# Ten projection steps beside the scan, window attention and latent keys beside latent attention, and low parts of weights by an adding DMA

## The chip, the cores and the metric

One core of a Trainium2 chip runs the whole kernel as one program. The metric is device time in microseconds, the median of three runs. The engines are named as the profile names them: PE (TensorE, matrix products), DVE (VectorE), ACT (ScalarE), POOL (GpSimd), and SP, whose queue issues most DMAs. POOL issues DMAs too.

## What is computed

A two-layer encoder over 1024 tokens of 1024 features, all in float32. Cut to what matters here:

```python
for i in range(DEPTH):
    u = h @ w_in[i]
    (cq, ckv, kr, hy_u, sq, sk, sv, ssd_z, ssd_xbc, ssd_dt) = jnp.split(u, IN_OFFSETS, axis=-1)
    y_a = mla_mixer(cq, ckv, kr, ...)          # latent attention
    y_b = hyena_mixer(hy_u, ...)               # short convolution, two long convolutions with gates
    y_c = swa_mixer(sq, sk, sv, swa_sink[i])   # window attention
    y_d = ssd_mixer(ssd_xbc, ssd_dt, ...) * jax.nn.silu(ssd_z)   # state-space scan with its gate
    y = group_rms_norm(jnp.concatenate([y_a, y_b, y_c, y_d], -1), mix_norm_g[i], 4)
    h = layer_norm(ALPHA * h + y @ w_out[i], ...)
    # then the MLP and a per-layer embedding, each with its norm
```

## The kernel before

Products are made in float32 of reduced width, three for one: an operand is split into a high part (ACT copies it with rounding) and a low part (the operand less its high part, on DVE or POOL), and a product is high x high, high x low, low x high. `split` at line 92 does that, `load_w` (line 112) loads a weight on SP into the tile `wraw` (two buffers) and splits it into `wh` and `wl` (tag `whl`, four buffers, so two pairs).

The input projection is done in tiles of 128 features (`in_proj`, line 564): 48 products of 128x128 by 128x512 each, into a PSUM tile of two banks (`pp`, two buffers). The tiles are cut into two steps each. `proj` in `mixers` runs through 20 of them: six for Hyena, five for the scan's inputs (the sixth was made at the head), SV, SK, two SQ for window attention, two CQ and one CKV for latent attention (`latent`, line 615, with a gain and sums of squares), and two gates Z. Each result goes to DRAM and is read again by its mixer.

A mixer is a Python generator, and `interleave` (line 43) emits several of them in step with one another, by the number of steps that is given beside each. The scheduler of the language then orders each engine's instructions, with that emission as its priority. Three stages follow one another in each layer, in `mixers` (line 579):

- Hyena (54 steps) beside the projection (42 steps); the projection's low parts are made by POOL.
- The scan `ssd` (44), window attention `swa` (32) and the keys and values of latent attention `mla_keys` (50, of which the first 34 do nothing).
- Latent attention `mla` (40) beside the first loads of the output projection (`out_ahead`, 36).

Memory between the stages is shared: pools are opened and closed as a stack, from the left and from the right, and a tile waits for the tiles that had its place. The eight tiles of 8 KB with the tag `X` hold the layer's input, as high and low parts, until the last projection tile is done. After that the scan's inputs and states (lines 824 to 832) and the latent keys `kT` take their place. Window attention scores, its transposed probabilities and latent attention's scores all use the PSUM tile of two banks.

Of the kernel before, what the change touches and what calls it, by code (L numbers as in the profile page):

```python
# [28 lines left out]
# columns of the packed per-layer parameters  # L29
# [4 lines left out]
# feature tiles of the input projection  # L34
# [8 lines left out]
def interleave(*flows):  # L43
    """Emits flows, each (generator, number of its steps), in step with one another."""
    live = [[g, 0, n] for g, n in flows]
    while live:
        f = min(live, key=lambda f: f[1] / f[2])
        try:
            next(f[0])
            f[1] += 1  # L50
        except StopIteration:
            live.remove(f)


def stagger(items):
    """Emits the stages of items so that each item is one stage behind the one before it."""
# [18 lines left out]
class Trunk:  # L75
# [16 lines left out]
    def split(self, hi, lo, src, eng=None):  # L92
        self.act(hi, src)
        self.tt(lo, src, r(hi), ALU.subtract, eng)

# [16 lines left out]
    def load_w(self, src, shape, pool=None, tag="whl", eng=None, bufs=None):  # L112
# [7 lines left out]
        self.split(hi, lo, raw, eng or nc.gpsimd)  # L120
        return hi, lo

# [23 lines left out]
    def to_x_after(self, x, H, t0, t1, ins, pair=False):  # L146
        """Transposes token tiles t0 to t1, once the products up to ins have freed the tiles that the
        result goes to."""
# [11 lines left out]
    def layer_norm(self, h, gb, eps=None, first=None):  # L160
        """The statistics; returns two functions that normalise h in place, one after the other."""
# [16 lines left out]
        def affine(c=512):  # L178
            """The first c columns, scaled already, on GpSimd, the others on VectorE."""
# [74 lines left out]
    def embed(self):  # L254
        """Normalises the input; the second half of the tokens only when the function that is returned runs."""
# [43 lines left out]
    def sin_of(self, fp, out, pre):  # L299
        """out = sin(pre) with the argument brought to [-pi, pi]."""  # L300
# [99 lines left out]
    def bruun(self, pool, zm, zp, C):  # L400
        """Residues of a polynomial of 1024 coefficients (8 blocks of 128 rows, C columns each)
        modulo the eight factors of x^2048 - 1 of degree 256; zm and zp are its residues modulo
        x^1024 - 1 and x^1024 + 1."""
# [36 lines left out]
    def conv_fft(self, l, n, pool, z, feature_major, out):  # L440
        """Circular convolution of z (token-major, 8 x 256) with filter n, and the skip term that the
        filter holds; the result is token-major [128, 8 * 256] or feature-major [128, 2, 8 * 128]."""
# [102 lines left out]
    def in_start(self, l, tile_i, eng=None):  # L545
# [5 lines left out]
        else:  # L551
            w = self.load_w(self.t["w_in"][l, tile_i], [128, 8, 128], eng=eng)
        return w, self.two()

    def in_half(self, x, w, ps, hf):
        c0 = hf * 512
        if not isinstance(w, tuple):
            # the products of the high and the low parts of the weights, in separate rows
# [5 lines left out]
    def in_proj(self, l, x, tile_i):  # L564
        """One tile of 128 features, [128, 1024] in PSUM, in two steps."""
        w, ps = self.in_start(l, tile_i)
# [6 lines left out]
    def conv3(self, out, ps, cw):  # L573
        """Centred 3-tap convolution along the free dim with bias: cw columns w0, w1, w2, b."""
# [4 lines left out]
    def mixers(self, l, x, mu, late, st0):  # L579
# [6 lines left out]
        res, sw = {}, ExitStack()  # L586
        ss = self.sm.tile([128, 4, 8], F32, name="ss")

        def scalars(su, ps):
            """Rotary key and dt, token-major."""  # L590
# [24 lines left out]
        def latent(pr, ti, k, rs, last, n):  # L615
            """A latent of attention with its gain, to DRAM; the sums of its squares go to rs."""
# [16 lines left out]
        def proj(pr, su, head, v, x1):  # L633
# [42 lines left out]
            for i in range(2):  # L676
                yield from plain(pr, T_SQ + i, qd[:, i])
                yield
            for i in range(2):
# [4 lines left out]
            yield from latent(pr, T_CKV, 2, res["rk"], True, 128)  # L684
            yield
            for i in range(2):
                yield from plain(pr, T_Z + i, zd[:, i], AF.Silu)
                yield
# [23 lines left out]
        with ExitStack() as ssu:  # L712
            with ExitStack() as st:
# [14 lines left out]
                interleave((hyena(st, v, x1), 54), (proj(pr, su, head, v, x1), 42))  # L728
            m1 = self.pool(st0, f"m1_{l}")
            w2 = self.pool(sw, f"w2_{l}", 2, side=RIGHT)  # L730
            att = {}
            with ExitStack() as st:
                mc = self.pool(st, f"mc{l}", 2)
                interleave((self.ssd(l, st, res["scal"], xbc, zd, yd[3]), 44), (self.swa(l, w2, yd[2], qd, kd, vd), 32),
                           (self.mla_keys(l, mc, m1, att, cd, res), 50))
            sw.close()
        rows, ahead = {}, {}
# [14 lines left out]
        with ExitStack() as sa:  # L752
            m2 = self.pool(sa, f"m2_{l}", 2)
            interleave((self.mla(l, m2, att, yd[0]), 40), (out_ahead(), 36))
        return yd, ss, rows, ahead

    def token_sums(self, sq):
        """Sums over features of the tiles sq [128 features, 512 tokens], as [128, 4] with tokens on partitions."""
# [5 lines left out]
    def squares(self, ss, g, hf, y, sq):  # L764
        """For the sums of squares of group g for 512 tokens, whose features are y, tokens on partitions:
        returns the function that finishes them on the tensor engine."""
# [6 lines left out]
    def ssd_scalars(self, l, mu, dtr):  # L773
# [5 lines left out]
        # softplus(x) = max(x, 0) + log1p(exp(-|x|)), the log by its series in e / (2 + e)  # L779
# [32 lines left out]
        # log(dt) - acs  # L812
# [6 lines left out]
    def ssd(self, l, ss, scal, xbc, zd, yd):  # L819
        nc = self.nc  # L820
        Ah, Al, lg, w, dec, dsum, eacs = scal
        res = {}
# [981 lines left out]
```

## Time and profile before

| | us |
|---|---|
| median of 3 runs | 3237.84 |
| lowest and highest run | 3234.51, 3241.9 |
| span of the profiled execution | 3236.6 |
| stage of Hyena and projection, first layer | 341 |
| stage of scan, window attention and keys | 137 |
| stage of latent attention | 135 |

An engine's busy time in a stretch is the time in which at least one of its instructions ran. The granted clock is a share of TensorE's full 2.4 GHz: 1.0 is full speed, 0.5 is its lower level, and a figure in between is a mean over the stretch.

### The profile page before, as it was taken

How to read it: one execution, taken by the hardware profiler on the slowest of the kernel's cores; microseconds unless marked ns; L12 is line 12 of the kernel's file. 1: busy time of each engine (PE TensorE's matmuls, PEld its weight loads, DVE VectorE, ACT ScalarE, POOL GpSimd, SP SyncE). 2: the span in 40 equal slices, each digit the busy share in tenths (PEclk: the TensorE clock that was granted, in tenths of full speed). 3: DMA queues.
4: the chain of work that ended last, by engine and by line, in shares of the span. 5: the costliest groups of instructions: out<-in, count | busy, mean ns of one | idle time of the engine just before them, and what ended most of it. 6: DMA issues, size and time to landing. Idle time of an engine off the chain costs nothing.

```text
span 3236.6 us, 40462 instructions
## 1 busy us (share of the span) xinstructions
PE 2976.9 (92%) x14316; PEld 2429.1 (75%) x14316; DVE 2451.0 (76%) x3711; ACT 1292.0 (40%) x2278; POOL 1821.3 (56%) x1371
## 2 busy tenths in 40 slices
PE   6999989998999999999989998899989999989996
PEld 4887866877777777777868877778777777767685
DVE  7678776878765557999777786778786555689986
ACT  4332365743333334333343323667333333343341
POOL 5455533527656556886435454345177555578855
PEclk9999998999999999999999998999999999999998
DMA  5566523022222225313335755130222222343232
GB/s 178 156 200 204 192 75 130 16 83 85 85 79 78 78 79 198 123 47 115 126 100 172 225 192 165 53 121 25 97 85 79 79 78 78 114 163 107 74 135 92
DMA packets 140468, 368.98 MB, mean 114 GB/s; under 512 B 15139, under 2 KB 42023, under 8 KB 140009
## 3 DMA queue, kind: packets, MB, share of 16 engines
q1 hardware_dynamic: 126008, 315.72, 28.8%
q0 software_dynamic: 14256, 50.67, 5.2%
q8 instruction: 114, 1.87, 0.2%
q14 instruction: 90, 0.73, 0.1%
HBM read 278.77 MB, written 87.56 MB: 113 GB/s over the span
## 4 chain that ended last, share of the span: by engine, by line
PE 39%; DVE 21%; POOL 16%; issue 10%; DMA 10%; ACT 4%; SPq 0%; POOLq 0%; DVEq 0%; ACTq 0%
PE ps L99 18%; PE pp L99 13%; POOL w L87 5%; DMA wraw<-in_ffn_w_gate_dram 4%; POOL wraw L87 4%; DVE part L87 3%; POOL u L87 2%; DVE fr L87 2%; POOL H L87 2%; PE ps L942 2%; DVE H L90 2%; DVE s L87 1%; POOL part L87 1%; DVE H L87 1%; DMA wraw<-in_ffn_w_up_dram 1%
## 5 line engine op out<-in xcount | busy, mean ns | idle before, releaser
L99 PE MATMUL ps<-x,w 128*128 128x512 f32 x2112 | 508.2, 394 | 11.3 <-ACT v L84 6.1
L99 PEld LDWEIGHTS ps<-x,w 128*128 128x128 f32 x2112 | 400.1, 190 | 99.1 <-ACT v L84 7.0
L99 PE MATMUL pp<-x,wh 128*128 128x512 f32 x1344 | 427.9, 397 | 1.8 <-ACT wh L84 1.8
L99 PE MATMUL ps<-xq,w 128*128 128x512 f32 x1584 | 391.1, 397 | 29.7 <-DVE u L87 24.3
L1582 PE MATMUL ps<-part 128*128 128x512 f32 x1440 | 351.2, 399 | 33.8 <-DVE H L87 10.8
L99 PEld LDWEIGHTS ps<-xq,w 128*128 128x128 f32 x1584 | 292.9, 188 | 117.2 <-DVE u L87 50.7
L1582 PEld LDWEIGHTS ps<-part 128*128 128x128 f32 x1440 | 270.9, 191 | 110.5 <-DVE H L87 20.3
L99 PEld LDWEIGHTS pp<-x,wh 128*128 128x128 f32 x1344 | 254.9, 192 | 54.3 <-ACT wh L84 2.0
L87 POOL TENSOR_TENSOR w<-wraw,w 128x512 fp32r<-128x512 f32 x164 | 217.5, 1345 | 116.0 <-ACT w L84 116.0
L99 PE MATMUL pp<-x,wl 128*128 128x512 f32 x672 | 266.5, 397 | 3.8 <-POOL wl L87 3.8
L84 ACT ACTIVATE w<-wraw 128x512 fp32r<-128x512 f32 x264 | 151.8, 622 | 268.0 <-DMA wraw<-in_ffn_w_up_dram 218.6
L87 POOL TENSOR_TENSOR wl<-wraw,wh 128x1024 fp32r<-128x1024 f32 (+2 forms) x61 | 152.8, 2507 | 182.7 <-ACT wh L84 124.2
L87 POOL TENSOR_TENSOR part<-fr,part 128x512 fp32r<-128x512 f32 x120 | 192.4, 1628 | 47.2 <-ACT part L84 42.2
L87 DVE TENSOR_TENSOR s<-wraw 128x512 f32<-128x512 f32 x44 | 55.4, 1259 | 202.2 <-DMA wraw<-in_ffn_w_gate_dram 199.8
L99 PE MATMUL ps<-wo,yn 128*128 128x512 f32 x768 | 189.7, 405 | 5.4 <-DVE H L90 3.0
L1039 POOL TENSOR_TENSOR P<-P,smr 128x1024 f32<-128x1024 f32 x64 | 121.1, 1893 | 112.2 <-DVE smr L1038 103.3
L99 PEld LDWEIGHTS ps<-wo,yn 128*128 128x128 f32 x768 | 147.1, 195 | 39.4 <-DVE H L90 4.8
L90 DVE SCALAR_TENSOR_TENSOR g<-g,pp 128x1023 f32<-128x1023 f32 x88 | 126.6, 1439 | 57.7 <-ACT g L84 57.7
L87 POOL TENSOR_TENSOR u<-u,g 128x512 f32<-128x512 f32 x44 | 78.7, 1788 | 152.5 <-ACT g L84 152.3
L87 DVE TENSOR_TENSOR part<-wr,part 128x512 fp32r<-128x512 f32 x124 | 158.2, 1299 | 4.8 <-ACT part L84 4.8
L99 PE MATMUL ps<-wh,x 128*128 128x512 f32 x512 | 158.8, 391 | 0.0
L99 PEld LDWEIGHTS pp<-x,wl 128*128 128x128 f32 x672 | 128.5, 191 | 30.5 <-POOL wl L87 4.7
(381 smaller groups left out, 7038.7 us busy)
## 6 DMA issues: line engine op xcount, KB each, us to landing
c_fwd<-in_c_fwd_dram POOLq DMA_DIRECT2D x64, 512.0 KB, 5.1
wraw<-in_ffn_w_up_dram SPq DMA_DIRECT2D x50, 512.0 KB, 3.5
wraw<-in_ffn_w_gate_dram SPq DMA_DIRECT2D x44, 512.0 KB, 4.5
f<-u SPq DMA_DIRECT2D x88, 256.0 KB, 2.0
wraw<-in_w_in_dram SPq DMA_DIRECT2D x42, 512.0 KB, 4.1
fr<-f SPq DMA_DIRECT2D x40, 512.0 KB, 4.5
wr<-in_ffn_w_down_dram SPq DMA_DIRECT2D x36, 512.0 KB, 6.4
c_inv<-in_c_inv_dram POOLq DMA_DIRECT2D x32, 512.0 KB, 5.0
```

The lines of the kernel that those rows point to most:

```text
L84: self.nc.scalar.activation(out, in_, func, **kw)
L87: (eng or self.nc.vector).tensor_tensor(out, a, b, op=op)
L90: return self.nc.vector.scalar_tensor_tensor(out, a, s, b, op0=op0, op1=op1)
L99: ins = self.nc.tensor.matmul(out, a, b, start=i == 0, stop=i == n - 1)
L942: ins = self.nc.tensor.matmul(out[0:64] if j else out, v[:, 0, :] if j else v.rearrange("p i d -> p (i d)"), terms[i][1 + j], start=k == 0 ...
L1039: nc.gpsimd.tensor_tensor(P, P, sm.to_broadcast([128, T]), op=ALU.mult)
L1582: nc.tensor.matmul(ps, u, v, start=k == 0 and (p != 1 or ch == 0), stop=k == 5 and (p != 1 or ch == last))
```

## The change

Three things are done.

- The five tiles Z, CKV and CQ (ten steps) leave `proj`, and a new flow `proj_late` (10) makes them beside the scan (44), the gates first. The scan's inputs and states get a pool of their own, since the tag `X` still holds the projection's operands.
- Window attention (now 44) and the latent keys, which are now the first part of a flow `attention` (48) with latent attention behind them, stand beside `out_ahead` (36). The 34 empty steps of `mla_keys` are gone.
- In all projection tiles but the first two of Hyena's, the low part is made without POOL's arithmetic: ACT writes the high part, then its negative into the low part's tile, and a DMA that POOL issues adds the weight to that from DRAM.

```diff
+    def split_added(self, hi, lo, src, far):
+        self.act(hi, src)
+        self.act(lo, src, scale=-1.0)
+        self.nc.gpsimd.dma_start(lo, far, accum_op=ALU.add)
@@ load_w(..., far=False)
-        self.split(hi, lo, raw, eng or nc.gpsimd)
+        if far:
+            self.split_added(hi, lo, raw, src)
+        else:
+            self.split(hi, lo, raw, eng or nc.gpsimd)
@@ in_proj
-        w, ps = self.in_start(l, tile_i)
+        w, ps = self.in_start(l, tile_i, far=tile_i not in (T_HY, T_HY + 1))
@@ mixers, end of proj
+        def proj_late(pr):
+            for i in range(2):
+                yield from plain(pr, T_Z + i, zd[:, i], AF.Silu)
+                yield
+            yield from latent(pr, T_CKV, 2, res["rk"], True, 128)
+            yield
             for i in range(2):
                 yield from latent(pr, T_CQ + i, i, res["rq"], i, 256)
                 yield
             rq = res["rq"]
             nc.vector.tensor_scalar(rq, rq, 96.0 ** -0.5, None, op0=ALU.mult)
-            yield from latent(pr, T_CKV, 2, res["rk"], True, 128)
-            yield
-            for i in range(2):
-                yield from plain(pr, T_Z + i, zd[:, i], AF.Silu)
-                yield
@@ mixers, the three stages
-                interleave((hyena(st, v, x1), 54), (proj(pr, su, head, v, x1), 42))
-            m1 = self.pool(st0, f"m1_{l}")
-            w2 = self.pool(sw, f"w2_{l}", 2, side=RIGHT)
-            att = {}
-            with ExitStack() as st:
-                mc = self.pool(st, f"mc{l}", 2)
-                interleave((self.ssd(l, st, res["scal"], xbc, zd, yd[3]), 44), (self.swa(l, w2, yd[2], qd, kd, vd), 32),
-                           (self.mla_keys(l, mc, m1, att, cd, res), 50))
-            sw.close()
+                interleave((hyena(st, v, x1), 54), (proj(pr, su, head, v, x1), 32))
+            with ExitStack() as st:
+                interleave((self.ssd(l, st, res["scal"], xbc, zd, yd[3]), 44), (proj_late(self.pool(st, f"pl{l}", 2)), 10))
         rows, ahead = {}, {}
+        def attention(mc, m1, m2):
+            att = {}
+            yield from self.mla_keys(l, mc, m1, att, cd, res)
+            yield from self.mla(l, m2, att, yd[0])
...
         with ExitStack() as sa:
+            w2 = self.pool(sa, f"w2_{l}", 2, side=RIGHT)
+            m1 = self.pool(sa, f"m1_{l}")
+            mc = self.pool(sa, f"mc{l}", 2)
             m2 = self.pool(sa, f"m2_{l}", 2)
-            interleave((self.mla(l, m2, att, yd[0]), 40), (out_ahead(), 36))
+            interleave((attention(mc, m1, m2), 48), (self.swa(l, w2, yd[2], qd, kd, vd), 44), (out_ahead(), 36))
@@ ssd
+        sb = self.pool(ss, f"sb{l}")
         for j in range(3):
-            pair = self.xp.tile([128, 2, T], F32, name="xbc", tag="X")
+            pair = sb.tile([128, 2, T], F32, name=f"xbc{j}")
...
-            prev.append(self.xp.tile([128, 8, 2, 128], F32, name="prev", tag="X"))
-            xt.append(self.xp.tile([128, 8, 2, 128], F32, name="xt", tag="X"))
+            prev.append(sb.tile([128, 8, 2, 128], F32, name=f"prev{g}"))
+            xt.append(sb.tile([128, 8, 2, 128], F32, name=f"xt{g}"))
@@ mla_keys
-        for _ in range(34):
-            yield
```

## Rows read from the trace of the kernel before

**Rows 1.** The page's part 1: busy time of each engine, share of the span.

```profile
PE 2976.9 (92%) x14316; PEld 2429.1 (75%) x14316; DVE 2451.0 (76%) x3711; ACT 1292.0 (40%) x2278; POOL 1821.3 (56%) x1371
```

**Rows 2.** Windows, by stage: stretch, length, busy us, clock, DMA share, GB/s.

```profile
core 0: us, PE busy (x) PEld busy (x) DVE busy (x) ACT busy (x) POOL busy (x), PEclk, DMA share, GB/s
62.00:403.00 341.00, 320.37 (x1694) 275.51 (x1694) 257.94 (x361) 115.08 (x164) 171.22 (x130) 0.96 0.57 183
403.00:540.00 137.00, 117.64 (x647) 90.19 (x645) 99.49 (x332) 84.94 (x255) 48.53 (x48) 0.93 0.25 79
540.00:675.00 135.00, 126.55 (x803) 110.47 (x803) 109.11 (x208) 92.06 (x167) 64.85 (x39) 0.95 0.19 67
1659.00:2000.00 341.00, 319.41 (x1691) 275.10 (x1690) 258.73 (x361) 115.10 (x164) 171.24 (x130) 0.96 0.57 182
```

**Rows 3.** Windows, three short stretches; columns as in rows 2.

```profile
520.00:560.00 40.00, 33.91 (x141) 23.34 (x141) 22.11 (x48) 20.80 (x43) 15.95 (x12) 0.79 0.61 220
560.00:660.00 100.00, 97.54 (x670) 87.90 (x669) 86.42 (x173) 74.56 (x138) 53.15 (x33) 1.00 0.06 15
300.00:350.00 50.00, 45.07 (x247) 39.18 (x246) 46.80 (x65) 15.04 (x22) 29.17 (x22) 0.93 0.56 184
```

**Rows 4.** Chain that ended last, 62 to 403 us: start, us, what.

```profile
310.92 5.52 DVE v L87 x2
...
389.37 13.72 PE pp L99 x60
```

**Rows 5.** Windows of the tile csq alone (the latents' sums of squares).

```profile
62.00:403.00 341.00, 6.61 (x48) 6.82 (x48) 3.54 (x6) 0.96 0.57 183
```

**Rows 6.** Groups by line on PE, 403 to 540 us: busy us, mean ns, idle before.

```profile
L99 PE MATMUL ps<-wpt,sV 128*64 128x256 f32 x88 | 22.9, 398 | 0.6 <-DVE prev L90 0.5
L885 PE MATMUL ps<-tri,s_Al 128*128 128x128 f32 x64 | 16.1, 287 | 0.0
...
L99 PE MATMUL ps<-wh,ck 128*128 128x512 f32 x16 | 7.1, 445 | 0.3 <-DVE V L90 0.3
...
L846 PE MATMUL ps<-ident,xbc 128*128 128x128 f32 x16 | 4.9, 304 | 0.0
```

**Rows 7.** Groups by line on DVE, 403 to 540 us.

```profile
L1131 DVE CUSTOM_DVE_ANT_0 ws<-pp,ab,pp 128x384 f32<-128x384 f32 (+1 forms) x32 | 17.5, 579 | 5.1 <-PE pp L99 5.0
...
L87 DVE TENSOR_TENSOR kT<-ps,kT 96x256 fp32r<-96x256 f32 x16 | 6.4, 417 | 3.0 <-ACT kT L84 3.0
...
L1142 DVE RECIPROCAL wsm<-wsm 128x2 f32<-128x2 f32 x16 | 2.5, 158 | 0.1
```

**Rows 8.** Groups by line on POOL and on ACT, 62 to 403 us.

```profile
L87 POOL TENSOR_TENSOR wl<-wraw,wh 128x1024 fp32r<-128x1024 f32 x20 | 51.8, 2588 | 51.3 <-ACT wh L84 51.3
...
L84 ACT ACTIVATE wh<-wraw 128x1024 fp32r<-128x1024 f32 x20 | 21.1, 1054 | 30.6 <-PE pp L99 27.9 <-issue 1.9 <-POOL kp L87 0.8
```

**Rows 9.** DVE groups, 62 to 403 us; then tile pa, ns min/median/max.

```profile
L87 DVE TENSOR_TENSOR pa<-pa,pb 128x256 f32<-128x256 f32 x32 | 29.5, 961 | 0.0
...
L87 DVE TENSOR_TENSOR t<-kp 128x512 f32<-128x512 f32 x2 | 5.8, 2878 | 0.0
...
L87 DVE TENSOR_TENSOR pa<-pa,pb x32: 412/420/2623, 247.3 to 369.3; 128x256 f32<-128x256 f32 x32
L87 DVE TENSOR_TENSOR pl<-pa,ph x16: 678/692/2110, 249.6 to 372.7; 128x512 fp32r<-128x512 f32 x16
```

**Rows 10.** Tile c_fwd, 62 to 403 us: POOL's casting loads of 512 KB.

```profile
L397 POOL DMA_DIRECT2D c_fwd<-in_c_fwd_dram x32: 527/573/910, 97.8 to 351.5; - x32
...
DMA to landing us min/median/max: 3.7/5.1/8.1
```

**Rows 11.** Timeline, POOL and PE: start, us, what [idle before].

```profile
174.71 2.56 POOL L87 TENSOR_TENSOR wl<-wraw,wh 128x1024 fp32r<-128x1024 f32 x1
...
183.44 0.39 PE L99 MATMUL pp<-x,wl 128*128 128x512 f32 x1
...
313.07 2.81 POOL L87 TENSOR_TENSOR wl<-wraw,wh 128x1024 fp32r<-128x1024 f32 x1
...
326.61 0.39 PE L99 MATMUL pp<-x,wl 128*128 128x512 f32 x1
```

More of the change, by code (lines that the diff above doesn't have):

```diff
@@ L110, in two, with load_w @@
         return self.ps2.tile([128, 1024], F32, name="pp", tag="pp")
-    def load_w(self, src, shape, pool=None, tag="whl", eng=None, bufs=None):
+    def load_w(self, src, shape, pool=None, tag="whl", eng=None, bufs=None, far=False):
         nc = self.nc
@@ L542, in conv_fft, with in_start @@
         out["y"] = st["ym"]
-    def in_start(self, l, tile_i, eng=None):
+    def in_start(self, l, tile_i, eng=None, far=False):
         if tile_i is None:
@@ L551, in in_start @@
         else:
-            w = self.load_w(self.t["w_in"][l, tile_i], [128, 8, 128], eng=eng)
+            w = self.load_w(self.t["w_in"][l, tile_i], [128, 8, 128], eng=eng, far=far)
         return w, self.two()
@@ L585, in mixers @@
         xbc = [dr(n, [128, 2, T]) for n in ("xs", "bs", "cs")]
-        res, sw = {}, ExitStack()
+        res = {}
         ss = self.sm.tile([128, 4, 8], F32, name="ss")
@@ L727, in mixers @@
                 x1 = hu.tile([128, 8, 256], F32, name="x1")
-                interleave((hyena(st, v, x1), 54), (proj(pr, su, head, v, x1), 42))
-            m1 = self.pool(st0, f"m1_{l}")
-            w2 = self.pool(sw, f"w2_{l}", 2, side=RIGHT)
-            att = {}
-            with ExitStack() as st:
-                mc = self.pool(st, f"mc{l}", 2)
-                interleave((self.ssd(l, st, res["scal"], xbc, zd, yd[3]), 44), (self.swa(l, w2, yd[2], qd, kd, vd), 32),
-                           (self.mla_keys(l, mc, m1, att, cd, res), 50))
-            sw.close()
-        rows, ahead = {}, {}
+                interleave((hyena(st, v, x1), 54), (proj(pr, su, head, v, x1), 32))
+            with ExitStack() as st:
+                interleave((self.ssd(l, st, res["scal"], xbc, zd, yd[3]), 44), (proj_late(self.pool(st, f"pl{l}", 2)), 10))
+        rows, ahead = {}, {}
+        def attention(mc, m1, m2):
+            att = {}
+            yield from self.mla_keys(l, mc, m1, att, cd, res)
+            yield from self.mla(l, m2, att, yd[0])
         def out_ahead():
```

## The prediction

> **What bounds the kernel now.** Read the busy lines of the page first [rows 1]: TensorE (PE) is busy for 92% of 3236.6 us, VectorE (DVE) for 76%, GpSimd (POOL) for 56%. An average says nothing of one stage, so the stretches are read next [rows 2]. The change touches three stages of each layer. A is Hyena beside the projection, 341 us; B is scan, window attention and latent keys, 137 us; C is latent attention, 135 us. The second layer repeats them to within 1 us each (its A is the fourth row; its B and C are 136 and 134 us). In A, PE is busy 320.4 us, idle 20.6; in B idle 19.4; in C 8.5. PE bounds A and C. B is bound by chains: no engine there reaches 90%, and the granted clock is down to 0.93, so part of it ran at the lower of the two levels. Then two of the short stretches [rows 3]: attention in full flow runs PE at 97.5% with DVE at 86%; the 40 us around its start have PE at 85% and a clock of 0.79. That start and B's chains are what there is to win; PE's work itself stays.
>
> **What is moved.** A chain piece [rows 4] has 60 products of the projection in 13.72 us, 0.229 us each. A tile is 48 of them, 11.0 us; five tiles (two gates Z, CKV, two CQ) are 54.9 us. The latents' sums of squares add 6.6 us of PE in a layer [rows 5]. So 61.5 us of PE a layer go from A to B. Window attention and keys go from B to C. The PE groups of B [rows 6] overlap: all 24 add up to 177.6 us where 117.6 is the busy time, so I scale by 0.66. The scan is ten groups, 16.1 us for the first listed, 4.9 for the last, 94.8 together: 62.8 scaled. Window attention is five groups (22.9, 13.4, 12.1, 10.5, 1.2): 39.8 scaled. Keys (7.1, 4.9, 3.2): 10.0. On DVE window attention is eight groups from 17.5 to 2.5 us, 44.7 in all, and keys two groups, 6.4 and 3.8 [rows 7].
>
> **The low parts.** Of 20 POOL subtractions in A, 18 a layer now become one more copy on ScalarE (ACT) and one adding DMA issued by POOL (13 in A, 5 moved to B). POOL loses 2.59 us each and gains an issue; ACT gains 1.05 us each, 19 us a layer on an engine at 34% [rows 2, 8]. What the subtraction costs is not its own time: POOL is idle half of A. It is what stands beside it on DVE. An addition of 256 columns takes 0.412 us at best, 0.961 in the mean and 2.62 at worst; a 512-column one of two SBUF operands averages 2.88 where its like needs 0.68 [rows 9]. Over the fourteen groups of that kind in A the excess over the shortest is 60 us (17.6 for the first row alone, 4.4 for the second). The subtractions are 51.8 us of some 130 us of POOL's tensor work there, 40%; 18 of 20 go: 60 x 0.4 x 0.9 = 22 us off DVE in A, 257.9 to 236.
>
> The adding DMA is in no row. The nearest is POOL's own casting load of the same 512 KB: issue 0.527 to 0.910 us, median 0.573, landing 3.7 to 8.1 us, median 5.1 [rows 10]. I take the median: it is the same queue and size. The low part is then ready 1.05 + 0.57 + 5.1 - 2.45 = 4.3 us later than today (2.9 to 7.6). The cover is read off the tiles [rows 11]: one subtraction runs from 174.71 to 177.27 and the first product that needs it comes at 183.44, 6.2 us in hand, the tightest of the 18; the other shown has 10.7, which is their median. So it costs nothing up to a landing of about 11.5 us, and with the cover gone each us is a us of PE per tile. The two tiles right behind the head keep the subtraction, since the first of them has no cover at all.
>
> The Trainium skill (DMA: Bandwidth & Descriptors, Rules for kernel authors) says that an accumulating DMA reads its destination and writes it later. No run here shows one. If that doubled the landing, an estimate is 10.2 us: still under the median cover, some 3 us a layer at the tightest tile. The skill's SBUF — State Buffer (SBUF: two separate sides) warns that a DMA from GpSimd waits for its descriptors while VectorE holds the shared port. The rows don't bear that out at a price: 32 issues beside a DVE 76% busy never took over 0.91 us [rows 10]; by the rule taken at its worst each of 36 waits for one 0.68 us instruction, and the cover hides it.
>
> **Queues passed.** SP issues five fewer loads and stores in A and five more in B, half a microsecond each; on POOL a far load that waits for ACT's second copy holds the splits and filter loads that stand behind it, as the subtraction does today (POOL sits 51.3 us of A waiting for the high part [rows 8]), 1 us longer each. I cost this at nothing in A, because the high part is made a whole tile ahead; without that cover it is 13 us a layer. The gates' Silu now stands beside the scan's exponentials: a table load or two on ACT, hidden, since ACT is at 62% of B [rows 2]. H's prefetch for the output projection, today at the start of C, must wait until window attention has left that memory, three quarters into C; a quarter of C, some 45 us, still covers it.
>
> **Stage A.** PE 320.4 - 61.5 = 258.9 us. With today's idle time, 279.5. DVE's 236 us would be 84% of that, against 76% now, so Hyena's own chains show more often: I add 7.5 and take 287. Ends: 269 (idle halved, because DVE is freed just where it was on the chain) and 312 (DVE's share stays at 76%: Hyena sets the pace). The densest 50 us of A have DVE at 94% [rows 3], which is nearer to the lower end.
>
> **Stage B.** Scan 62.8 + 61.5 = 124.3 us of PE with DVE and POOL light. Products with no chain of their own fill the scan's waits; I take 126. Ends 124 and 139 (15 of today's 19.4 us idle stay). The scan's tiles move from the operands' memory to Hyena's, so the wait for the last projection tile becomes one for Hyena's last store; the gates' products run meanwhile.
>
> **Stage C.** PE 126.6 + 39.8 + 10.0 = 176.4 us; DVE 109.1 + 44.7 + 10.2 = 164. At 97.5% [rows 3], 181. Its start is late: the values' tile lies where the scan's output lay, so keys wait for the scan's last store. Against today's start (6.1 us idle in 40, clock 0.79) window attention fills some; I add 8 and take 189. Ends 181 and 203 (DVE no better than its 81% of C today: 164 / 0.81).
>
> **Sum.** 287 + 126 + 189 = 602 against 613: 11 us a layer, 22 in all. The profiled span of 3236.6 becomes 3214.6. The median of the runs is 1.2 us over that span; the forecast is 3215.8. Everything else in the layer (output projection, MLP) is untouched.
>
> **Rivals.**
> 1. Freeing DVE pays more than its share, because the excess falls on Hyena's chain (two results beside POOL take 5.5 us together at 310.9, against 1.4 [rows 4, 9]). A 272, B 125, C 183: 33 a layer, 3172. Chance 0.13. Against it: fewer products are left to fill A.
> 2. C finds a new bound: window attention and latent attention share DVE and the two double-bank PSUM buffers. C 203, sum 616, 3244. For it: DVE at 86% already without window attention. Chance 0.17.
> 3. Slower, one mechanism: Hyena's chain paces A. It decides where its DVE share can't rise above 76%. A 312, sum 627: 28 us lost, 3266. Against it: DVE ran at 94% for 50 us. Chance 0.09.
> 4. Low parts late. It decides at a landing of 11.5 us; at 13, 1.5 us for each of 36 tiles is 54 us: 3270. Chance 0.09.
> 5. The change doesn't do what it says: the scan can't start until Hyena's memory is free, and the five tiles run ahead of it, not beside. B 137, sum 613: 3238. Chance 0.07.
>
> **How the numbers follow.** The forecast has 0.45. The ends of all three stages at once would be 3160 and 3320; they are unlikely together. Leaving out half of rival 1 and most of 3 and 4 (0.2), the range is 3172 to 3262. A change of 0.2% (6.5 us) is about what a measurement of this kernel can tell. Faster: 0.43 of the forecast, 0.13, 0.03 of rival 2: 0.59. Same: 0.02, 0.06, 0.06 of rival 5: 0.14. Slower: 0.08 of rival 2, 3 and 4 whole, 0.01 of 5: 0.27.
>
> **What would show it.** In the profile after: A near 287 with DVE busy near 236 and the additions' mean near 0.5 us; the far loads' landing under 10 us and no PE wait for wl; B's PE over 95%; C near 189 with PE over 90%. Wrong it is if A keeps over 300, if PE waits for DMA wl, or if C passes 200 with DVE at its limit or PE waiting for exponentials to free the double banks.

## The result, and the profile after

The changed kernel takes 3316.7 us (median of four runs, 3315.3 to 3323.5) against 3236.2 us of the kernel before: a ratio of 1.0252, 95% interval 1.0232 to 1.0273. It is 2.5% slower, some 80 us; 3215.8 us had been forecast. The profiled execution spans 3316.3 us.

The page's part 1 after, to be held against [rows 1]:

```profile
PE 2998.0 (90%) x14316; PEld 2439.2 (74%) x14316; DVE 2390.2 (72%) x3711; ACT 1329.1 (40%) x2314; POOL 1755.0 (53%) x1371
```

The three stages of both layers after, as windows with the columns of [rows 2]: A, B, C, then A, B, C of the second layer. They begin and end at the same events as there.

```profile
63.00:396.00 333.00, 290.54 (x1528) 247.03 (x1528) 219.71 (x350) 122.88 (x169) 131.06 (x125) 0.94 0.70 202
396.00:495.00 99.00, 91.36 (x482) 76.52 (x482) 47.92 (x158) 40.41 (x124) 13.82 (x20) 0.91 0.30 94
495.00:711.00 216.00, 191.90 (x1135) 158.16 (x1134) 171.08 (x392) 147.19 (x312) 106.01 (x72) 0.94 0.23 71
1692.00:2034.00 342.00, 293.74 (x1530) 249.42 (x1528) 216.70 (x350) 122.99 (x169) 130.48 (x125) 0.94 0.67 196
2034.00:2135.00 101.00, 92.60 (x482) 76.62 (x482) 48.62 (x158) 40.40 (x124) 14.08 (x20) 0.91 0.28 90
2135.00:2355.00 220.00, 191.94 (x1137) 156.86 (x1137) 168.81 (x392) 148.14 (x312) 105.66 (x72) 0.94 0.23 70
```

B and C are 99 + 216 = 315 us, to the us what the forecast gave them together (126 + 189), and 321 in the second layer. The miss is A: 333 and 342 us, where 287 was forecast and 341 stood before. TensorE (PE) has 166 fewer products in it than before (1528 against 1694 in [rows 2]), and A is hardly shorter: PE's busy time fell by 29.8 us, not by the 61.5 of the forecast, and its idle time went from 20.6 to 42.5 us.

Where that idle time lies: three short stretches of A (windows, same columns), then what PE waited for in 345 to 400 us (engine, line, what: us in all, times, longest).

```profile
232.00:260.00 28.00, 28.00 (x137) 23.60 (x136) 22.57 (x37) 11.64 (x14) 10.85 (x11) 1.00 1.00 310
260.00:300.00 40.00, 40.00 (x254) 36.34 (x253) 26.55 (x46) 15.58 (x24) 19.27 (x20) 1.00 0.91 279
...
345.00:396.00 51.00, 27.28 (x140) 23.70 (x140) 32.70 (x48) 10.88 (x20) 19.84 (x18) 0.74 0.50 154
```

```profile
PE ps L861 <- DMA xbc<-xs: 10.3, 1, 10.3
PE ps L105 <- DMA c_inv<-in_c_inv_dram: 6.1, 1, 6.1
PE pp L105 <- ACT cv L84: 3.2, 1, 3.2
PE ps L105 <- DVE pl L87: 1.9, 1, 1.9
```

PE is full from 232 to 300 us. Then the projections run out. Two gate tiles run ahead of the scan (their products begin at 306 and 327 us), but their results' memory lies in Hyena's place, so they sit in both double PSUM banks until Hyena lets go: the two copies that empty the banks start at 378.2 and 379.1 us, and the third late tile waits for the first of them.

```profile
378.23 1.92 ACT L84 ACTIVATE cv<-pp 128x1024 f32<-128x1024 f32 x2
```

From 345 to 379 us PE has only Hyena's own products, and after them 22 products of the third late tile: 27 us of work in 51, and the granted clock falls to 0.74. The scan's inputs are loaded after Hyena's last store, and PE waits 10.3 us for them.

Hyena itself ends hardly earlier. Its last store (tile y, issue of the two halves; columns: ns min/median/max, first and last start) is at 387.6 us; before, it was at 390.4.

```profile
L719 SPq DMA_DIRECT2D y<-x x2: 555/584/612, 387.6 to 388.3; - x2
```

### The profile page after: what moved, and what is told of

It is laid out like the page before. It is cut to its first block, busy times and chain, and to the rows that moved or that the text cites. A ratio compares the mean times of both kernels' runs of the same rounds, so it can differ in the third digit from the quotient of the medians.

```text
span 3316.3 us, 40489 instructions
## 1 busy us (share of the span) xinstructions
PE 2998.0 (90%) x14316; PEld 2439.2 (74%) x14316; DVE 2390.2 (72%) x3711; ACT 1329.1 (40%) x2314; POOL 1755.0 (53%) x1371
## 4 chain that ended last, share of the span: by engine, by line
PE 20%; DVE 12%; POOL 9%; DMA 6%; issue 6%; ACT 2%; POOLq 0%; SPq 0%; DVEq 0%; ACTq 0%
PE ps L105 9%; PE pp L105 6%; DMA wraw<-in_ffn_w_gate_dram 2%; POOL w L87 2%; POOL wraw L87 2%; DVE part L87 2%; POOL H L87 2%; DVE H L90 1%; PE ps L1490 1%; DVE H L87 1%; PE ps L1595 1%; POOL u L87 1%; DVE fr L87 1%; DMA c_fwd<-in_c_fwd_dram 1%; DVE E L87 1%
## 5 line engine op out<-in xcount | busy, mean ns | idle before, releaser
L105 PE MATMUL pp<-x,wh 128*128 128x512 f32 x1344 | 437.5, 402 | 17.5 <-DVE cv L90 9.3
L84 ACT ACTIVATE part<-fr 128x512 fp32r<-128x512 f32 x120 | 70.7, 624 | 177.8 <-PE ps L1595 78.4
```

Of the source, the lines that this page charges most:

```text
L84: self.nc.scalar.activation(out, in_, func, **kw)
L105: ins = self.nc.tensor.matmul(out, a, b, start=i == 0, stop=i == n - 1)
```

## The experiments

Theory 1 was that the moves cost: memory handed from stage to stage makes barriers of what used to overlap, and the products that filled A are used up early. Theory 2: the mix of windowed and latent attention is bound by VectorE (DVE) or the double banks. Theory 3: the adding DMA costs. A fourth is rival 3 of the prediction: Hyena's own chain of dependent steps sets A, whatever PE has to do.

The table holds every kernel to the same two spans of each layer, read from the timelines: A* from the first rotary key to the issue of Hyena's last store, R* from there to the last store of latent attention. Median, ratio to the kernel before with its 95% interval, then A* and R* in us (layer 1 / layer 2). Each ratio is to runs of the kernel before that were made beside it (their medians are 3233.1 to 3236.8 us); each pair of spans is from one profiled execution.

| kernel | median us | ratio | A* | R* |
|---|---|---|---|---|
| before | 3236.2 | | 328.1 / 328.6 | 283.6 / 281.4 |
| after | 3316.7 | 1.0252 (1.0232 to 1.0273) | 324.0 / 332.6 | 322.5 / 327.9 |
| e1_low_parts | 3210.9 | 0.9930 (0.9914 to 0.9947) | 324.4 / 321.5 | 279.0 / 277.1 |
| e2_moves | 3329.4 | 1.0295 (1.0273 to 1.0318) | 332.4 / 325.0 | 327.1 / 325.5 |
| e4_attn_moved | 3265.4 | 1.0091 (1.0066 to 1.0116) | 330.9 / 327.3 | 293.2 / 293.9 |
| e5_shared | 3283.8 | 1.0156 (1.0140 to 1.0172) | 327.7 / 322.3 | 312.0 / 310.7 |
| e6_keys_room | 3303.6 | 1.0221 (1.0192 to 1.0250) | 322.8 / 319.8 | 324.0 / 319.9 |
| e8_no_window | 3203.8 | 0.9917 (0.9892 to 0.9943) | 320.5 / 322.5 | 273.3 / 272.7 |
| e9_no_cover | 3255.2 | 1.0065 (1.0045 to 1.0086) | 301.1 / 291.7 | 328.0 / 320.0 |
| e11_more_low_parts | 3232.0 | 0.9993 (0.9976 to 1.0010) | 322.7 / 319.0 | 282.8 / 279.1 |
| e12_five_fewer | 3172.3 | 0.9807 (0.9787 to 0.9827) | 312.5 / 313.8 | 265.3 / 267.7 |
| e13_thirteen | 3168.5 | 0.9794 (0.9778 to 0.9811) | 313.8 / 311.6 | 265.6 / 268.9 |

**The parts of the change, one by one.** The low parts alone:

```diff
 (kernel before, with split_added, load_w, in_start of the change)
-        w, ps = self.in_start(l, tile_i)
+        w, ps = self.in_start(l, tile_i, far=tile_i not in (T_HY, T_HY + 1))
```

> The kernel before with one part of the change alone: the low parts of the projection's weights come by the adding DMA, for all tiles but the two at the head of the Hyena group and the two products ahead of the stage; no step is moved. Theory 1 (the loss of the change lies in its moves: the memory of one stage is given to the next, so the stages no longer overlap, and the products that could have filled in are used up early): the adding DMA costs nothing, VectorE has some 30 to 38 us less to do in each Hyena stage, and the stage is no longer than before; 3200 to 3240 us. Theory 3 (the adding DMA itself is what costs, because its weights land later or its traffic slows other transfers): slower than before, 3255 us or more, with TensorE waiting for wl.

The moves alone:

```diff
 (changed kernel)
-        w, ps = self.in_start(l, tile_i, far=tile_i not in (T_HY, T_HY + 1))
+        w, ps = self.in_start(l, tile_i, far=False)
```

> The changed kernel with its low parts made by GpSimd again, so the two moves alone. Theory 1 (the moves cost, through stages that no longer overlap): 3305 to 3340 us, as the changed kernel or a little more, with TensorE idle for some 30 us at the end of the Hyena stage. Theory 3 (the adding DMA costs): 3280 us or less.

Attention's move alone:

```diff
 (kernel before)
-                interleave((self.ssd(...), 44), (self.swa(...), 32), (self.mla_keys(...), 50))
+                run(self.ssd(l, st, res["scal"], xbc, zd, yd[3]))
...
-            interleave((self.mla(l, m2, att, yd[0]), 40), (out_ahead(), 36))
+            interleave((attention(mc, m1, m2), 48), (self.swa(...), 44), (out_ahead(), 36))
```

> The kernel before with one move alone: windowed attention and the latent keys beside latent attention; all projections stay in the Hyena stage, the scan stands alone with its tiles where they were, low parts by GpSimd. Theory 1: the Hyena stage keeps its 341 us; the scan alone has no cover and takes 75 to 95 us; the stage of latent attention takes the 216 us of the changed kernel or up to 15 less, since its start still waits for the scan's memory: together 620 to 650 us against 613, so 3250 to 3310 us. Theory 2 (the mix of windowed and latent attention is bound throughout by VectorE and the two double banks, not at its start): that stage takes 210 us or more with TensorE idle spread evenly over it, more than 10% in its middle 100 us too.

Theory 3 falls as the cause of the loss: alone, the adding DMA makes the kernel 0.7% faster, and without it the moves cost 2.95%. (VectorE's relief in A is 24.8 us, less than the 30 to 38 expected.) Attention's move alone costs 29 us (3265.4 against 3236.2); the projection's move on top of it costs 64 more (3329.4). In e4_attn_moved the three stages of layer 1 are 332, 71 and 222 us, 625 together as theory 1 had it, but the scan alone is shorter than its 75 to 95 us and attention's stage longer than its 201 to 216. The projection's move is the worst and also the plainest: from e4_attn_moved to e2_moves the five tiles are moved out of A (the two gate tiles run ahead into it again, so PE's busy time in A* falls by 15 us only, 310.4 to 295.3), A* stays (330.9 to 332.4, 327.3 to 325.0), and R* grows by 34 and 32 us.

The adding DMA in e1_low_parts, A of layer 1 (tile wl; ns min/median/max of the issue, then the landing), and the one row of PE's waits, over the whole kernel, that names it:

```profile
L115 POOL DMA_DIRECT2D wl<-in_w_in_dram x18: 875/888/950, 83.5 to 380.4; - x18
```

```profile
PE pp L99 <- DMA wl<-in_w_in_dram: 5.4, 3, 2.5
```

**Does the memory make the barrier?** First the late tiles' results, given room beside Hyena:

```diff
 (changed kernel)
                 su = self.pool(ssu, f"su{l}", side=RIGHT)
+                pr = self.pool(ssu, f"pr{l}", 2)
                 hu = self.pool(st, f"hu{l}")
-                pr = self.pool(st, f"pr{l}", 2)
...
-                interleave((self.ssd(...), 44), (proj_late(self.pool(st, f"pl{l}", 2)), 10))
+                interleave((self.ssd(...), 44), (proj_late(pr), 10))
```

> The changed kernel with one difference: the five late projection tiles take their results' memory from the pool of the early ones, which is opened ahead of Hyena's, in place of a pool of their own in Hyena's place; no instruction is added or taken away. Theory 1: the gates' and the key latent's products leave PSUM while Hyena still runs, TensorE's idle stretch at the end of the Hyena stage (some 30 us of a layer) shrinks by 15 to 25 us in each layer, and the time falls to 3265 to 3290 us. Theory 2 (attention's mix is the loss): no more than 10 us fall, 3305 us or more.

3283.8 us, 33 less than the changed kernel and within theory 1's bounds. That the late tiles were held by their results' memory is shown: the copies that empty the two gates' banks now start at 323.3 and 347.0 us, well before Hyena's last store at 391.8.

```profile
323.34 1.00 ACT L84 ACTIVATE cv<-pp 128x1024 f32<-128x1024 f32 x1
...
346.97 1.01 ACT L84 ACTIVATE cv<-pp 128x1024 f32<-128x1024 f32 x1
```

The gain is not where it was expected to show, though: R* is 10.5 and 17 us shorter (1596 products are done when Hyena ends in layer 1, in place of 1528); A* is no shorter in layer 1 and 10 us shorter in layer 2. Some of the gain is lost behind Hyena: with less work left to fill in, PE waits up to 16.0 us for the scan's inputs, in place of 10.3. Then the keys' room:

```diff
 (changed kernel)
+            m1 = self.pool(st0, f"m1_{l}")
+            mc = self.pool(st0, f"mc{l}", 2)
             with ExitStack() as st:
                 interleave((self.ssd(...), 44), (proj_late(self.pool(st, f"pl{l}", 2)), 10))
...
-            m1 = self.pool(sa, f"m1_{l}")
-            mc = self.pool(sa, f"mc{l}", 2)
```

> The changed kernel with one difference: the memory for the latent keys and values lies ahead of the scan's tiles in place of inside them, so the keys need not wait for the scan's last tile. Theory 1 (the stages stand apart because memory is handed on): the first softmax tile of a layer comes 10 to 20 us earlier after the scan, TensorE's 7.8 us wait for Q at the start of that stage goes, 3280 to 3300 us. Rival (the start is a chain of its own: latent load, split, keys, queries, first scores): the start stays and the time with it, 3308 us or more.

3303.6 us, 13 less and between the two expectations, but not by the mechanism: the first softmax tile of layer 1 comes at 551.7 us against 552.2, 69 us after the scan's last decay tile (Lm) against 65. PE's longest wait for Q in that start falls from 7.8 to 2.6 us and others take its place (4.2 us for `ws`, a tile of windowed attention). The keys' memory is not what holds C's start.

**Is C bound by its mix?** Windowed attention left out:

```diff
 (changed kernel)
-            w2 = self.pool(sa, f"w2_{l}", 2, side=RIGHT)
+            nc.sync.dma_start(yd[2], qd)
...
-            interleave((attention(mc, m1, m2), 48), (self.swa(...), 44), (out_ahead(), 36))
+            interleave((attention(mc, m1, m2), 48), (out_ahead(), 36))
```

> The changed kernel without windowed attention: its output is replaced by a copy of its queries, so the result is not the reference's; the stage of latent attention holds keys, latent attention and the weights ahead only. TensorE's own work in windowed attention is about 40 us of a layer (88 products of 0.216 us, 48 of 0.18 and 88 transposes of 0.109, and the mask's). If TensorE's work sets that stage's length (theory 1), the stage falls by 35 to 45 us from 216 to about 175, the time to 3230 to 3250 us. If the mix is bound by VectorE or the double banks (theory 2), it falls by 60 us or more of a layer, 3200 us or less.

From the scan's last decay tile to attention's last store in layer 1, windows, the changed kernel and then this one:

```profile
487.00:710.00 223.00, 198.43 (x1159) 163.23 (x1159) 177.42 (x410) 147.87 (x317) 107.90 (x75) 0.93 0.24 74
```

```profile
482.00:656.00 174.00, 150.40 (x913) 126.86 (x912) 129.53 (x262) 108.56 (x216) 80.43 (x57) 0.92 0.22 69
```

The time, 3203.8 us, lies between the two expectations (10 us of it are layer 2's A*, 322.5 for 332.6); the rows decide. The stretch falls by 49 us, PE's busy time in it by 48.0: us for us. The 40 us of the expectation left out part of that work. Theory 2 falls: in attention's full flow (552 to 700 us after) PE is busy for 137.8 of 148 us. The double banks cost a little there: PE waits 10.2 us for them (for P, 5.4 and 1.3, and for wmx, 3.5), where before, in all of C, it waited 4.9 for P. What the mix does cost more is the start: 65 us from the scan's last decay tile to the first softmax tile with windowed attention, 50 without it.

**What sets A?** The changed kernel without nine of its thirteen tiles in A, then the kernel before without the five tiles that the change moves, with GpSimd's subtractions and with the adding DMA:

```diff
 (e9_no_cover: changed kernel)
             for i in range(1, 6):
-                yield from ssd_in(i)
+                nc.sync.dma_start(xbc[i // 2][:, i % 2], t["w_in"][l, i]...)
...
-            yield from plain(pr, T_SV, vd)            (and T_SK, T_SQ, T_SQ + 1)
+                nc.sync.dma_start(d, t["w_in"][l, i]...)
 (e12_five_fewer, e13_thirteen: kernel before)
-                yield from latent(pr, T_CQ + i, i, res["rq"], i, 256)
+                nc.sync.dma_start(cd[:, k], t["w_in"][l, k]...)
-                yield from plain(pr, T_Z + i, zd[:, i], AF.Silu)
+                nc.sync.dma_start(zd[:, i], t["w_in"][l, i]...)
```

> The changed kernel without nine projection tiles of the Hyena stage (five inputs of the scan and the windowed queries, keys and values are copied from the weights instead), so the result is not the reference's; nine times 13.7 us = 123 us of TensorE's work of a layer are gone from that stage and nothing of Hyena's own. If TensorE's work sets the length of the stage, as the forecast took it, the stage falls from 324 us (first rotary key to Hyena's last store) to 200 to 240 us and the time to 3150 us or less. If Hyena's own chain of dependent steps sets it, the stage keeps 285 us or more, and the time is 3240 us or more.

> The kernel before without its five last projection tiles (the latents' and the gates' values are copied from the weights and the latents' scales set to one, so the result is not the reference's): 68.6 us of TensorE's work are gone from the Hyena stage of each layer, with five of its 18 subtractions, and nothing else changes. If TensorE's work and its usual idle time set the stage, as the forecast's first term took it, the stage falls from 328 us (first rotary key to Hyena's last store) to some 270 us and the time to 3100 to 3130 us. If Hyena's own chain sets it, the stage keeps 305 us or more, and the time is 3180 us or more.

> The kernel before without its five last projection tiles and with the low parts by the adding DMA, so the Hyena stage holds just what the changed kernel leaves in it, and no late tile can run ahead into it (not the reference's result, for the same reason). The forecast put this stage at 287 us in its own bounds, 270 to 275 us between the marks used here. Hyena's chain: 300 us or more, and no more than 10 us below the same kernel with GpSimd's subtractions; the late tiles that ran ahead had then taken nothing from it.

These expectations took 13.7 us for a tile. That piece of the chain holds 60 products and a tile 48 [rows 4]: nine tiles are 99 us, the five 61.5 with their sums. The verdict on A* stands all the same. With 99 us of PE taken from a layer, A* of the changed kernel falls by 23 and 41 us; with 61.5 us taken from the kernel before, by 15.6 and 14.8. In e9_no_cover PE is busy for 71% of A* (213.4 of 302 us), and A* is still 301 and 292 us. PE's work is not without weight: PE's busy time in A* fell by 77 and 85 us there, by 40.6 and 40.5 in e12_five_fewer, so each us of it that went took 0.3 to 0.5 us off A*.

The time of e12_five_fewer, 3172.3 us, is below the 3180 or more that was expected if Hyena's chain sets A, because R* falls too, by 18.3 and 13.7 us. The kernel before, then e12_five_fewer, A* and R* of layer 1:

```profile
62.00:391.00 329.00, 308.37 (x1641) 265.58 (x1641) 253.79 (x359) 111.94 (x161) 166.14 (x124) 0.96 0.56 178
391.00:674.00 283.00, 255.19 (x1496) 209.80 (x1495) 212.26 (x541) 179.15 (x424) 118.46 (x94) 0.94 0.25 84
```

```profile
61.00:374.00 313.00, 267.80 (x1422) 231.35 (x1420) 240.95 (x351) 104.53 (x153) 152.41 (x123) 0.92 0.58 185
374.00:639.00 265.00, 239.82 (x1428) 197.32 (x1429) 211.43 (x541) 173.06 (x416) 115.00 (x88) 0.95 0.22 72
```

In the kernel before, the last projection tiles ran past Hyena's last store, to 403 us (the chain's piece at 389.37 in [rows 4]). Without the tiles that end is gone, and R* has 15.4 us less of PE's work. So leaving the five tiles out wins 64 us in all, 32 of a layer's 61.5, about half of it in A*.

The two halves of A* in e9_no_cover (cut at 232 us; the filters come first, then the two convolutions), and the first half of e13_thirteen and of the changed kernel:

```profile
66.00:232.00 166.00, 139.05 (x697) 115.96 (x696) 101.92 (x165) 61.04 (x85) 62.23 (x60) 0.89 0.65 184
232.00:368.00 136.00, 74.31 (x399) 68.26 (x399) 116.26 (x175) 30.46 (x53) 60.23 (x57) 0.68 0.49 151
```

```profile
62.00:230.00 168.00, 160.76 (x817) 135.13 (x818) 108.57 (x168) 71.91 (x94) 63.00 (x61) 0.97 0.69 194
```

```profile
63.00:232.00 169.00, 155.31 (x803) 129.52 (x804) 100.46 (x164) 72.05 (x95) 59.42 (x59) 0.99 0.66 185
```

The first half takes 166 to 169 us whether PE is at 84%, 92% or 96%. (Up to the filters' last store it is 161.1 us in e9_no_cover, 164.6 in e13_thirteen and 167.6 in the changed kernel.) The convolutions take 136 us with PE 55% busy. What they wait for is seen in the groups by line on PE of e9_no_cover, all of A (busy us, mean ns, then idle before them and what ended it), and in a piece of its timeline:

```profile
L105 PE MATMUL ps<-rh,c_fwd 128*128 128x256 f32 x256 | 65.2, 335 | 29.5 <-ACT rh L84 20.2 <-DMA c_fwd<-in_c_fwd_dram 9.2
...
L105 PE MATMUL ps<-ph,c_inv 128*128 128x256 f32 x64 | 17.2, 352 | 20.0 <-ACT ph L84 14.3 <-DMA c_inv<-in_c_inv_dram 5.6
L105 PE MATMUL ps<-c_inv,ph 128*128 128x256 f32 x64 | 16.2, 349 | 11.6 <-ACT ph L84 5.8 <-DMA c_inv<-in_c_inv_dram 4.5 <-DVE pb L87 1.3
```

```profile
234.58 3.57 DVE L90 SCALAR_TENSOR_TENSOR l<-v,t 128x512 f32<-128x512 f32 x1 [2.65 <-POOL t L87]
...
242.00 0.69 DVE L87 TENSOR_TENSOR pa<-ps,kt 128x512 f32<-128x512 f32 x1
...
243.87 0.76 DVE L87 TENSOR_TENSOR pa<-pa,pb 128x256 f32<-128x256 f32 x2
...
244.66 0.63 ACT L84 ACTIVATE ph<-pa 128x512 fp32r<-128x512 f32 x1 [5.09 <-DVE pa L87]
...
245.34 0.58 PE L105 MATMUL ps<-ph,c_inv 128*128 128x256 f32 x1 [6.81 <-ACT ph L84]
```

A spectrum passes from PE to DVE (multiplied, added), to ScalarE (high part) and back to PE, and PE's 6.8 us of idle time is that round. PE's longest wait is between the two convolutions, and for those 18 us DVE is busy for 17.54:

```profile
305.68 1.19 PE L105 MATMUL ps<-rh,c_fwd 128*128 128x256 f32 x2 [17.93 <-ACT rh L84]
```

```profile
287.70:305.70 18.00, 0.07 (x2) 0.02 (x1) 17.54 (x17) 1.42 (x4) 12.22 (x7) 0.50 0.26 87
```

DVE is busy for 116 of the 136 us. So in the convolutions the chain runs over DVE, and PE's other products mostly fill its gaps. PE's lower clock is not what keeps them long: an estimate from the means of `rh,c_fwd` (348 ns there, 296 before) is 11 us at most, 74.3 x (1 - 296 / 348). What sets the 166 us of the filters was not taken apart.

Between e12_five_fewer and e13_thirteen (3172.3 and 3168.5 us) no difference can be told: with thirteen tiles in A, taking 18 us off DVE there (240.95 to 223.05) brings nothing. The convolutions are 146 us in both (columns as before), DVE busy for 124.03 and 114.48 of them, so it is not DVE's busy time as such that sets them. That it is the steps in the rounds, and which of them, is argued and not shown:

```profile
228.00:374.00 146.00, 109.28 (x612) 97.43 (x610) 124.03 (x187) 41.57 (x68) 73.02 (x62) 0.86 0.66 210
```

```profile
230.00:376.00 146.00, 104.73 (x599) 92.40 (x597) 114.48 (x184) 45.13 (x71) 66.74 (x62) 0.87 0.73 221
```

**Further along the line that paid.** The low parts alone, with the MLP's weights added:

```diff
 (e1_low_parts; part() of the MLP takes far as in split_added)
-                a12 = part(w2, self.wp, "whl", eng)
+                a12 = part(w2, self.wp, "whl", eng, None if f is None else t["ffn_w_up"][l, f][:, 4:8])
...
-                w22 = part(a22, hp, "H")
+                w22 = part(a22, hp, "H", far=t["ffn_w_gate"][l, f][:, 4:8])
```

> The kernel of the low parts alone (3210.9 us), with the adding DMA also for the three parts of each MLP weight block that are used as they come from memory (first two of up, second of gate; not for the three blocks whose first products run ahead). If GpSimd's subtractions are a load there as they were in the projection (they hold VectorE back and end TensorE's waits), 3170 to 3205 us. If the stage is bound by TensorE alone, 3205 to 3215 us. If the low parts land too late for the products, slower: 3220 us or more.

3232.0 us: 21 us slower than e1_low_parts, as fast as the kernel before. GpSimd has 39 us less to do in the stretch of the MLP's features, but PE's products wait longer for DVE, here over the whole kernel, e1_low_parts and then this one:

```profile
PE ps L99 <- DVE u L87: 23.3, 39, 1.1
```

```profile
PE ps L99 <- DVE u L87: 45.3, 41, 2.5
```

No wait for the added parts shows, so "they land late" is not borne out either. Why DVE's u comes later stays open.

## Why the prediction was wrong

**Stage A is the step that failed.** It took PE's work and added today's idle time: 320.4 - 61.5 + 20.6 = 279.5, then 7.5 for chains. But PE's work did not set A's length us for us; most of it filled a stage that a chain set. The step said that A falls by 54 us. With the five tiles gone altogether A* is 312.5 to 313.8 in layer 1, so there were 15 us to win between its marks, and some 13 in the projection's end behind Hyena's last store (390.4 to 403 us), which the forecast counts in A. The changed kernel did not win even those. Of the 61.5 us of PE only 29.8 left A, since the two gate tiles and part of a third ran ahead into it, and the rest of the miss is idle time, 42.5 us in place of 28.1. A* is 324.0 and 332.6, 10 and 21 us above e13_thirteen, which has the same thirteen tiles and no late ones that could run ahead. Of that, 7 and 9 us lie behind the filters' last store, where the late tiles are; the filters, 3 and 12 us longer, were not traced. That PE was 94% busy in A [rows 2] showed how well A was filled, not what bounded it.

**Rival 3 named the mechanism and sized it wrongly.** "Hyena's chain paces A" gave 312 us, because it let DVE's share stand at 76% and so let A shrink with DVE's work. The share fell: 219.7 of 333 us, 66%. The chain includes hand-offs between engines and a first half in which DVE is busy for 100 of 169 us, and it kept its length when DVE was relieved (e12_five_fewer to e13_thirteen). With A at 333 and the forecast's own B and C the rival would have given 648 us a layer, what layer 1 measured. The argument against it, DVE at 94% for 50 us [rows 3], was rather a sign for it: that stretch lies in the convolutions.

**The low parts: sizes right, worth wrong.** 22 us were to go off DVE in A; with all 18 tiles in place it is 24.8 (253.8 us before, 229.0 in e1_low_parts, over A*; in the changed kernel DVE has 219.7 us in A, where 236 was forecast), and the additions' mean is 0.587 us after, from 0.961 [rows 9]:

```profile
L87 DVE TENSOR_TENSOR pa<-pa,pb 128x256 f32<-128x256 f32 x32 | 17.5, 587 | 0.0
```

A* became 4 and 7 us shorter by it, R* 4.5 each: with all tiles in place the relief is worth something; with thirteen it is not. Why, and where R*'s share comes from, was not traced. The landing (tile wl after, 62 to 410 us) was taken at 5.1 us:

```profile
DMA to landing us min/median/max: 5.4/7.1/10.8
```

All of it is under the 11.5 us at which rival 4 decides, and PE waits for wl 0.8 us in all after. Rival 4 falls. The issue is dearer, 0.89 us in place of 0.57. The prediction's estimate of a doubled landing was too high: the casting load of the same size beside it lands in 5.9 us, so the adding one takes 1.2 times that. The Trainium skill (DMA: Bandwidth & Descriptors, Rules for kernel authors) says that an accumulating DMA reads its destination and writes it later. No run shows that reading by itself; the landing is 1.2 us longer here.

**B and C: right in sum, each off by 27 us.** B came out at 99 in place of 126, since two of the five tiles had run in A, as rival 5 has it (it put B at 137). The scan's 62.8 us, scaled from overlapping groups, hold: alone in e4_attn_moved it has 62.94 us of PE, in a stage of 71 us:

```profile
399.00:470.00 71.00, 62.94 (x366) 51.81 (x364) 43.93 (x145) 34.08 (x113) 12.68 (x21) 1.00 0.30 102
```

C came out at 216 in place of 189: PE is busy for 191.9 us where 176.4 was forecast, and idle for 24.1 in place of 12.6. Windowed attention's work was mis-sized, 48 us for 39.8. Latent attention's first queries were left out of the sum: before, they ran in B (the products of wh,cn, wl,cn, qs and kT,qT there, 2.7 + 1.3 + 1.9 + 0.8 = 6.7 us, 4.4 by the prediction's scale), and all of them stand in C now. And the start was: 8 us were added, and it is 65 us long where it was 43 before (Lm's last at 504.4, the first softmax tile at 547.6). Rival 2's mechanism, a bound by DVE or the banks, is not what made it long; e8_no_window shows PE's work, us for us. That two errors cancel in B + C is luck. "Products with no chain of their own fill the scan's waits" was true of A and B as they stood before: windowed attention and keys were such products, and moving them cost R* 10 and 12 us with the projection untouched (e4_attn_moved).

**Queues passed** were rightly put at nothing for PE: its waits for high parts (1.8 us) and for GpSimd's splits (3.8) are what they were. For DVE they were not nothing: with the adding DMA the loads of Hyena's decay table `dec` come later. DVE's waits for them in the first half of A, layer 1, before and in e1_low_parts:

```profile
DVE hk L87 <- DMA dec<-in_c_decay_dram: 7.3, 3, 4.7
```

```profile
DVE hk L87 <- DMA dec<-in_c_decay_dram: 16.5, 5, 7.8
```

Over the whole kernel this wait is 12.5 to 16.2 us in the four kernels without the adding DMA (before, e2_moves, e4_attn_moved, e12_five_fewer) and 23.4 to 37.1 in the eight with it. That it lengthens A is not shown. Two costs were missed at A's end: PE's 10.3 us for the scan's inputs, whose memory is Hyena's, and some 6 us for a load of `c_inv`, once in a layer, for which it never waited before. The second goes with PE running short of other products: it is 15.4 us in e12_five_fewer, which moves nothing, and 0.2 in e5_shared (both layers). For the first the prediction had "the gates' products run meanwhile"; they had run already, and were held in PSUM. Before, these inputs were loaded no earlier (from 395 us), but the projection's last tile kept PE busy to 403.

**Over the layer**: A* -4 and +4, R* +39 and +46.5; 35 and 50.5 us, some 85 in all, and the rest of the kernel a few us shorter.

## What to carry to other kernels

A stage whose busiest engine is at 94% may still be set by a chain, when much of that engine's work is filler: before moving work out, leave it out in an experiment and see how far the stage and the kernel shrink; that is all a move can win, here 15 us of the stage and 32 of a layer for 61.5 us of work, before the work costs anything where it lands. A filler is best left where chains leave gaps, and moved work costs its whole time where it lands, as windowed attention's 48 us did. If work is moved to a later stage, see that its results have memory that is free early; else it runs ahead and blocks the buffers that it sits in.

Of the kernels run, the low parts alone, with nothing moved, beat both: 3210.9 us, 0.7% under the kernel before.

## What the runs showed of the hardware

The clock followed PE's idle time into a stage that a chain bounds: in the convolutions of e9_no_cover, with PE busy for 55% of the time, the granted clock is 0.68 (a mix of the 1.2 and the 2.4 GHz level), against 0.95 in the same stretch before with PE at 93%. Work taken off PE was given back in part by slower products: the mean of `rh,c_fwd` in that stretch is 348 ns, against 296. Before, then e9_no_cover:

```profile
228.00:391.00 163.00, 151.35 (x835) 133.07 (x834) 137.42 (x195) 49.11 (x76) 86.82 (x63) 0.95 0.58 192
L99 PE MATMUL ps<-rh,c_fwd 128*128 128x256 f32 x128 | 27.7, 296 | 4.4 <-ACT rh L84 4.4
```

```profile
L105 PE MATMUL ps<-rh,c_fwd 128*128 128x256 f32 x124 | 33.2, 348 | 19.1 <-ACT rh L84 17.9 <-DMA c_fwd<-in_c_fwd_dram 1.0
```

No issue of the adding DMA was held up beside a busy DVE: the 18 in A of e1_low_parts took 0.875 to 0.950 us, a spread of 9%. Other loads were slower beside it: the decay table's took up to 8.1 us to land in e1_low_parts, 3.9 before, and the mean busy share of the DMA engines in A* was 0.72, from 0.56.
